# Both halves of the input projection as one sequence, and the squares of x summed on TensorE

## Chip, cores and metric

One core of a Trainium2 chip runs the whole program. The metric is the device time of one execution, in microseconds (us). Of the kernel before there are three timed runs and one execution taken apart by the hardware profiler.

## What is computed

One layer of a decoder for 2048 tokens of width 1024, all in float32. Cut to what the change touches:

```python
u = rms_norm(h, attn_pre_norm)                  # mean of squares over the 1024 features of a token
c_q, c_kv, k_rope, m_q, m_k, m_v, m_o, m_i, m_f = split_cols(u @ w_in, IN_SIZES)
q  = rms_norm(c_q, q_norm) @ w_uq               # low-rank queries: 4 heads of 128 + 64 (rotary)
kv = rms_norm(c_kv, kv_norm) @ w_ukv            # low-rank keys and values
mla_out = causal_mla(q, k, v)                   # softmax attention
hm = mlstm_chunkwise(mq, mk, m_v, m_i, m_f)     # matrix memory with gates
mix = concat(mla_out, sigmoid(m_o) * hm) @ w_out
# residual, a dense gated FFN, a gated per-layer embedding
```

`rms_norm` divides a token's row by the root of its mean square and multiplies by a gain. The product `u @ w_in` is the input projection; the change is in it and in the work beside it.

## The kernel before, in words

Every float32 operand is split into a high and a low part (float32r), and a product is three matmuls, `mm3` (L143, L144, L145: high by high, low by high, high by low). In the trace `xh` and `xl` are the two parts of tokens, `wh` and `wl` those of weights; ScalarE makes the high part (L135), VectorE the low one (L131). `ps` is a PSUM bank of large products, `psx` one of the three banks for small work.

Tokens come in two halves of 1024, each of two blocks of 512. Output rows come in 18 blocks of 128; two row blocks and two token blocks are one pair. A pair is done straight in 96 matmuls of 512 columns, or by Strassen's seven products in 84, for which sums of token operands and of weights are made first. Phase 1 runs so:

- `lead`: the first four row blocks of the first half (the latents), 192 straight matmuls on x that is not yet normalised. Meanwhile the squares of x are added up: ScalarE squares a tile (L264), VectorE adds it to `ct` or `acc` (`square_sum`), and when eight tiles are in, four one-column products with the constant `rmean` give the mean for 512 tokens (`rms_begin`, L169). A chain of eleven small VectorE operations on 128x4 numbers makes the root (L171, L152 to L157), four transposes on TensorE spread it (`rms_end`, L177), ScalarE copies it to `acc`, and the latents are multiplied by it (L720). Only then may the x operands be normalised (`unit`, L641).
- `project(0)`: one straight pair and seven Strassen pairs, 684 matmuls of 512 columns. Beside it `next_stats` adds up the squares of the second half.
- the seam: `lead_first` and `lead_second` load, normalise and sum the second half's x.
- `project(1)`: one straight pair and nine Strassen pairs.

Work beside the products is a list of steps, `side`; one step is taken after each twelve matmuls (`tick`). `beside` is a second list, taken from at every second tick. Steps are `rope_steps` (sines of the positions), `keys_values` (two steps: load, normalise, turn and store a block of the low-rank keys), `query_weights` and `value_weights` (products of weight matrices), and `queries` (20 steps for two token blocks: load, normalise, weights, products, `put` into DRAM, at the end the rotary parts, stored to `q_r`). A scheduler then puts the program into a fixed order for each engine. SP's queue issues nearly all loads and stores, in order. Where a matmul waits, all later ones wait behind it. Tiles come from pools: five of `ld`, four of `wr`, seven of `wh` and of `wl`, one of `sq`.

Phase 2 (attention and mLSTM) follows, with `gates` (scans on the gate rows, which go through DRAM: `g_ag`, `g_ar`, `g_md`, `g_bias`) already started in phase 1. Phase 3 is the FFN. It already has a stream of several halves: the operands of a later half are summed by `x_sums` on VectorE, stored to DRAM (`h1op`) and loaded back by `fed` (L381) as the last pair of the half before needs them no more.

Of the kernel before, what the change touches and what calls it, by code (L numbers as in the profile page):

```python
# [17 lines left out]
P = 128  # L18
D = 1024
T = 2048  # L20
TB = 512
# [41 lines left out]
class Layer:  # L63
# [109 lines left out]

    def along(self, ps, y):
# [29 lines left out]

    def run_later(self):
# [22 lines left out]
    def behind(self):  # L228
        return self.after("PE")

# [175 lines left out]
    def strassen(self, xo, pairs, emit, lead, place=None, late=False):  # L406


        self.stream([self.job(pairs, emit, xo=xo, lead=lead, place=place, late=late)])
# [12 lines left out]
    def stream(self, jobs):  # L422
# [206 lines left out]
    def phase1(self):  # L629
        nc, a, V = self.nc, self.a, self.vecs  # L630
        st = ExitStack()
        with st:
# [13 lines left out]
            def next_x(k, t, alt=False, tag=None):  # L646
                return self.load(a["xT"][k, :, (2 + t) * TB:(3 + t) * TB], alt, tag)

            scale = {}

            def next_stats():
# [15 lines left out]

            self.side = [lambda f=f: behind(f) for f in rest] + 21 * [lambda: None] + self.keys_values(0) + self.query_weights()
            halo = self.project(0, self.ops, None, next_stats(), self.xs)
            self.until(lambda: 1 in scale)  # L670
            get = lambda k, t, tag: unit(next_x(k, t, k >= 4, tag), k, scale[t])
            self.lead_first(get)
            self.lead_second(get)
            self.project(1, self.ops, halo, None, self.xs)

    def lead(self, unit):
# [24 lines left out]
        def arrive(t, k):  # L701
# [4 lines left out]
            if k == 0:  # L706
                acc[t] = self.tl("ct")
            if k or t:
                self.square_sum(acc[t], x, k == 0, tag="acc")

        def begin(t):
            y[t] = self.rms_begin(g, acc[t], 1024)
# [12 lines left out]
        for t in range(2):  # L725
# [5 lines left out]
            for k in range(KD):  # L731
# [6 lines left out]
                for i in range(n):  # L738
                    if t == 0 and k % 4 == 0:
                        w[i, k // 4] = weight(i, k // 4)  # L740
                        if (i, k) == (0, 0):
                            self.square_sum(acc[t], x, True)
# [1032 lines left out]
```

## Time and profile before

| | us |
|---|---|
| median of 3 runs | 2706.18 (2705.91 to 2708.95) |
| the profiled execution | 2700.7 |
| its span in the trace | 2698.9 |
| PE busy | 2572.0 (95%) |
| DVE busy | 1971.9 (73%) |
| ACT busy | 1365.5 (51%) |
| granted clock, mean | 0.978 |

The span leaves 1.8 us of its execution outside; the execution is 5.5 us below the median. PE is TensorE, DVE is VectorE, ACT is ScalarE, POOL is GpSimd, SP is the queue that issues loads and stores. In the slices of the page PE is under 90% in the first five fortieths of the span, in the eighth and ninth, and in the last two. A matmul of 512 columns starts every 0.227 us at the full granted clock.

### The profile page before, as it was taken

Reading aid. Unit: us, or ns where it says so; the run is one execution under the profiler, and the core shown is the slowest. Engines: PE = TensorE matmul, PEld = TensorE weight load, DVE = VectorE, ACT = ScalarE, POOL = GpSimd, SP = SyncE. Lnnn points to the kernel's source line nnn. Section 1 sums busy time; section 2 is a strip of 40 time slices with the busy share of each in tenths; the row PEclk is TensorE's granted clock in tenths of the full one; section 3 lists DMA queues with packets and bytes.
Section 4 is the critical chain, followed back from the end, with each engine's and each line's share of the span. In section 5 each row is a group of like instructions: output and inputs, shape, how many; then the busy total and the mean of one; then the engine's idle time right before and its main releaser. Section 6 shows DMA issues by size and latency. Waiting matters only on the chain.

```text
span 2698.9 us, 36867 instructions
## 1 busy us (share of the span) xinstructions
PE 2572.0 (95%) x12019; PEld 2129.2 (79%) x12019; DVE 1971.9 (73%) x3635; ACT 1365.5 (51%) x2671; POOL 186.1 (7%) x393
## 2 busy tenths in 40 slices
PE   7799889989999999999999999999999999999978
PEld 5678678778888878878888888888888888787867
DVE  8987877566666662799787778676667678877885
ACT  5565565465555553465433354343446445356453
POOL 0010010153333200000000000000000000000000
PEclk9899899999999999999999999999999999999989
DMA  4345444743334133836566578662347567887853
GB/s 144 122 158 192 130 144 147 224 144 102 106 103 110 55 130 113 281 121 223 175 214 224 190 263 288 206 234 94 109 162 233 184 223 266 300 278 250 305 168 97
DMA packets 278845, 486.61 MB, mean 180 GB/s; under 512 B 32476, under 2 KB 54108, under 8 KB 278652
## 3 DMA queue, kind: packets, MB, share of 16 engines
q1 hardware_dynamic: 277308, 483.23, 54.5%
q8 instruction: 94, 1.54, 0.2%
q10 hardware_dynamic: 1344, 1.03, 0.1%
q14 instruction: 99, 0.81, 0.1%
HBM read 321.73 MB, written 162.40 MB: 179 GB/s over the span
## 4 chain that ended last, share of the span: by engine, by line
PE 79%; DMA 8%; DVE 6%; ACT 3%; issue 2%; POOL 1%; SPq 1%; ACTq 0%; DVEq 0%; POOLq 0%
PE ps L143 22%; PE ps L145 21%; PE ps L144 21%; PE ps_t L1400 2%; DMA wr<-g_rd 1%; PE ps_o L144 1%; DVE xl L131 1%; PE ps_s L1360 1%; PE ps_o L145 1%; DVE ct L131 1%; PE ps_o L143 1%; PE ps_s L1361 1%; PE ps_s L1362 1%; PE ps_s L1363 1%; PE psx L143 1%
## 5 line engine op out<-in xcount | busy, mean ns | idle before, releaser
L143 PE MATMUL ps<-xh,wh 128*128 128x512 f32 x2904 | 1141.6, 396 | 61.6 <-ACT wh L135 20.0
L144 PE MATMUL ps<-xl,wh 128*128 128x512 f32 x2904 | 1141.8, 393 | 3.7 <-DVE xl L131 1.9
L145 PE MATMUL ps<-xh,wl 128*128 128x512 f32 x2904 | 1140.2, 393 | 3.8 <-DVE wl L131 3.8
L143 PEld LDWEIGHTS ps<-xh,wh 128*128 128x128 f32 x2904 | 551.7, 190 | 185.9 <-ACT wh L135 21.8
L145 PEld LDWEIGHTS ps<-xh,wl 128*128 128x128 f32 x2904 | 551.0, 190 | 122.6 <-DVE wl L131 6.6
L144 PEld LDWEIGHTS ps<-xl,wh 128*128 128x128 f32 x2904 | 552.3, 190 | 120.5 <-DVE xl L131 3.4
L135 ACT CAST wh<-wr 128x512 fp32r<-128x512 f32 x346 | 214.5, 622 | 325.9 <-PE ps L144 204.1
L131 DVE TENSOR_TENSOR wl<-wr,wh 128x512 fp32r<-128x512 f32 x346 | 238.2, 690 | 157.8 <-ACT wh L135 154.5
L131 DVE TENSOR_TENSOR ct<-ps,ct 128x512 f32<-128x512 f32 x242 | 166.6, 689 | 92.7 <-PE ps L145 89.4
L382 ACT CAST wh<-wl 128x512 fp32r<-128x512 f32 (+1 forms) x217 | 128.3, 594 | 196.5 <-DMA wl<-w_sums_down 114.4
L131 DVE TENSOR_TENSOR wl<-wl,wh 128x512 fp32r<-128x512 f32 (+1 forms) x217 | 140.9, 656 | 100.4 <-ACT wh L382 99.5
L131 DVE TENSOR_TENSOR xl<-xl,xh 128x512 fp32r<-128x512 f32 x234 | 155.3, 689 | 22.8 <-ACT xh L382 21.1
L135 ACT CAST wh<-st 128x512 fp32r<-128x512 f32 x118 | 72.1, 622 | 160.4 <-PE ps L144 104.5
L382 ACT CAST xh<-xl 128x512 fp32r<-128x512 f32 x210 | 128.2, 622 | 42.8 <-DMA xl<-hfop 27.5
L1411 DVE TENSOR_TENSOR acc<-ps_t,acc 128x512 fp32r<-128x512 f32 (+2 forms) x144 | 91.8, 643 | 53.7 <-ACT acc L1410 53.2
L1368 DVE TENSOR_REDUCE mx<-ps_s 128x1 f32<-128x512 f32 (+3 forms) x160 | 97.0, 608 | 36.5 <-PE ps_s L1364 34.2
L467 ACT COPY ct<-ps 128x512 f32<-128x512 f32 x198 | 115.1, 581 | 13.5 <-PE ps L145 13.4
L1410 ACT CAST acc<-ps_t 128x512 fp32r<-128x512 f32 (+2 forms) x144 | 78.1, 552 | 69.5 <-PE ps_t L1400 67.7
L1378 ACT ACTIVATE xl<-ps_s,mn 128x512 f32<-128x512 f32 (+3 forms) x144 | 90.4, 634 | 40.3 <-DVE mn L1374 22.8
L131 DVE TENSOR_TENSOR wl<-st,wh 128x512 fp32r<-128x512 f32 x118 | 80.8, 688 | 11.6 <-ACT wh L135 11.6
L1400 PE MATMUL ps_t<-ident,xl 128*128 128x128 f32 x544 | 88.2, 276 | 0.3 <-DVE acc L1411 0.3
L1568 ACT ACTIVATE ct<-ct 128x512 f32<-128x512 f32 x88 | 55.7, 633 | 51.7 <-DVE ct L131 51.7
(342 smaller groups left out, 3353.5 us busy)
## 6 DMA issues: line engine op xcount, KB each, us to landing
xl<-hfop SPq DMA_DIRECT2D x154, 256.0 KB, 4.8
wl<-w_sums_down SPq DMA_DIRECT2D x112, 256.0 KB, 3.2
wr<-w_gate SPq DMA_DIRECT2D x88, 256.0 KB, 3.1
wr<-w_up SPq DMA_DIRECT2D x88, 256.0 KB, 3.5
wr<-w_in SPq DMA_DIRECT2D x80, 256.0 KB, 3.0
ld<-y SPq DMA_DIRECT2D x56, 256.0 KB, 4.3
wl<-w_sums_ple SPq DMA_DIRECT2D x49, 256.0 KB, 4.3
y<-ct SPq DMA_DIRECT2D x46, 256.0 KB, 3.2
```

The costliest lines, as they stand in the source:

```text
L131: (self.nc.gpsimd if eng == "pool" else self.nc.vector).tensor_tensor(out=out, in0=x, in1=y, op=op)
L135: self.nc.scalar.copy(out=hi, in_=src)
L143: mm(out, w[0], x[0], start=start, stop=False)
L144: mm(out, w[0], x[1], start=False, stop=False)
L145: mm(out, w[1], x[0], start=False, stop=stop)
L382: self.nc.scalar.copy(out=hi[:, :n], in_=raw)
L467: nc.scalar.copy(out=c, in_=bank)
L1368: v.tensor_reduce(mx[:, j, c:c + 1], s_ps[:, :w], axis=AX.X, op=ALU.max, negate=True)
L1378: nc.scalar.activation(out=p[:, :x.shape[1]], in_=x, func=AF.Exp, bias=top, accum_out=sm[:, j, c:c + 1])
L1400: nc.tensor.transpose(t_ps[:, j * P:(j + 1) * P], pt[j, kt // 4][:, kc], self.ident)
L1410: nc.scalar.copy(out=ph[:, b0:], in_=t_ps[:, c0:])
L1411: v.tensor_tensor(pl[:, b0:], t_ps[:, c0:], ph[:, b0:].bitcast(F32), ALU.subtract)
```

## The change

Phase 1 alone changes, in four ways.

1. Squares of x. `mean_square` lets ScalarE square a tile into `sq` and TensorE multiply it by `rmean` at once, four products of one column, added up in PSUM over eight tiles. There are 32 such groups of four instead of 4. VectorE's 28 additions of squares of x are gone. The sums for the latents stay as they were.
2. One sequence. `project` returns a job, and `stream` runs both. The second half has no straight pair and no operands of its own making at the seam: `next_sums` normalises its x, makes the Strassen sums on VectorE (32 large operations), stores 28 tiles of 256 KB in DRAM (`x_op`), and `fed` (L405 in the changed file) loads each back, 14.7 MB in all both ways, in place of the loads of sixteen tiles of x. Twelve matmuls of 512 columns are gone.
3. Finer steps. `keys_values` has six steps, `query_weights` ten and now runs first, `value_weights` one more, and `queries` takes 14 steps for a token block (with pauses 17 for the first half) in place of ten, each issuing less. Idle steps ahead are 14, not 21.
4. The end. What is left of `side` when the sequence is over is run then.

```diff
+    def mean_square(self, st, src, k, n):
+        sq = self.tl("sq")
+        self.nc.scalar.activation(out=sq, in_=src, func=AF.Square)
+        for j in range(4):
+            self.nc.tensor.matmul(st[:, j:j + 1], sq[:, j * P:(j + 1) * P], self.rmean[n], start=k + j == 0, stop=k == KD - 1,
+                                  skip_group_check=True)
...
                 while not jb["ready"]():
-                    if self.side:
-                        self.side.pop(0)()
+                    for work in (self.side, self.beside):
+                        if work:
+                            work.pop(0)()
                     self.run_soon()
                     self.run_later()
...
+            def next_sums(kk):
+                b = [unit(next_x(k, t), k, scale[t]) for k in (kk, 4 + kk) for t in range(2)]
+                self.x_sums(*b, x_op[kk], b[1], self.tl("sq"))
+                fed.append(kk)
+            def scaled(r, t):
+                scale[t] = r
+                if len(scale) == 2:
+                    self.beside += self.spaced([lambda kk=kk: next_sums(kk) for kk in range(4)], 2)
             def next_stats():
                 for t in range(2):
-                    acc = self.acc_tile()
+                    st = self.aux()
                     for k in range(KD):
-                        self.square_sum(acc, next_x(k, t), k == 0, "dve")
-                        yield
-                    self.rms_later(acc, 1024, lambda r, t=t: scale.__setitem__(t, r), lag=3)
+                        self.mean_square(st, next_x(k, t), k, 1024)
+                        if k % 3:
+                            yield
+                    self.rms_soon(st, lambda r, t=t: scaled(r, t))
...
-            self.side = [lambda f=f: behind(f) for f in rest] + 21 * [lambda: None] + self.keys_values(0) + self.query_weights()
-            halo = self.project(0, self.ops, None, next_stats(), self.xs)
-            self.until(lambda: 1 in scale)
-            get = lambda k, t, tag: unit(next_x(k, t, k >= 4, tag), k, scale[t])
-            self.lead_first(get)
-            self.lead_second(get)
-            self.project(1, self.ops, halo, None, self.xs)
+            self.side = [lambda f=f: behind(f) for f in rest] + 14 * [self.idle] + self.query_weights() + self.keys_values(0)
+            first, halo = self.project(0, None, next_stats(), xo=self.ops, lead=self.xs)
+            second, _ = self.project(1, halo, None, feed=lambda i: [x[i] for x in x_op], ready=lambda: len(fed) == 4)
+            self.stream([first, second])
+            while self.side:
+                self.tick()
...
-            if k or t:
-                self.square_sum(acc[t], x, k == 0, tag="acc")
...
+                if k == 0:
+                    acc[t] = self.aux()
+                for kk in [k] if t == 0 else range(2 * k, 2 * k + 2) if k < 4 else []:
+                    self.mean_square(acc[t], x0[kk, t], kk, 1024)
...
-            steps += [lambda: fetch(0), lambda t=t: normalise(t), weight]
+            pause = [] if tb else [self.idle]
+            steps += [lambda: fetch(0), lambda t=t: normalise(t), weight] + pause
             for i0 in range(2):
-                for i in range(2):
-                    steps.append(lambda b=b, i0=i0, i=i: (self.put(product(i), self.q_n[b][2 * i0 + i], tb),
-                                                          fetch(i0 + 1) if i == 0 else weight()))
+                put = [lambda b=b, i0=i0, i=i: self.put(product(i), self.q_n[b][2 * i0 + i], tb) for i in range(2)]
+                steps += [lambda i0=i0: fetch(i0 + 1), *put, weight] + pause
             steps += [lambda t=t: rotary(t, 0), lambda t=t: rotary(t, 1), lambda t=t: rotate(t)]
```

TensorE in the lead, around the transposes that spread the first root (`nrm_y`). Before:

```order
L144 MATMUL ps<-xl,wh 128x512
L145 MATMUL ps<-xh,wl 128x512
L177 MATMUL psx<-ident,nrm_y 128x128 x4
L169 MATMUL psx<-rmean_76,ct 128x1 x4
L143 MATMUL ps<-xh,wh 128x512
```

After:

```order
L144 MATMUL ps<-xl,wh 128x512
L145 MATMUL ps<-xh,wl 128x512
L184 MATMUL psx<-rmean_76,sq 128x1 x12
L190 MATMUL psx<-ident,nrm_y 128x128 x4
L184 MATMUL psx<-rmean_76,sq 128x1 x4
L143 MATMUL ps<-xh,wh 128x512
```

The transposes stand behind 120 large matmuls in both. Now three groups of one-column products, the last of the first block among them, stand right ahead of them.

VectorE, from the first root to the first multiplication of the latents by it (`ct<-ps,acc`). The part of before begins at the root's first operation:

```order
L171 TENSOR_SCALAR nrm_m<-psx 128x4
L131 TENSOR_TENSOR ct<-ct,acc 128x512
L737 SCALAR_TENSOR_TENSOR xl<-ld,vecs,xh 128x512
L1041 SCALAR_TENSOR_TENSOR raw<-raw 128x512
L737 SCALAR_TENSOR_TENSOR xl<-ld,vecs,xh 128x512
L152 TENSOR_SCALAR nrm_y<-nrm_m 128x4
L131 TENSOR_TENSOR ct<-ct,acc 128x512
L131 TENSOR_TENSOR wl<-wr,wh 128x512
L1041 SCALAR_TENSOR_TENSOR raw<-raw 128x512
L154 TENSOR_TENSOR nrm_b<-nrm_y 128x4
```

After:

```order
L131 TENSOR_TENSOR wl<-wr,wh 128x512 x2
L176 TENSOR_SCALAR nrm_m<-psx 128x4
L152 TENSOR_SCALAR nrm_y<-nrm_m 128x4
L154 TENSOR_TENSOR nrm_b<-nrm_y 128x4
L156 SCALAR_TENSOR_TENSOR nrm_b<-nrm_b,nrm_m 128x4
L157 SCALAR_TENSOR_TENSOR nrm_y<-nrm_b,nrm_y 128x4
L154 TENSOR_TENSOR nrm_b<-nrm_y 128x4
```

The large operations that stood inside the chain stand ahead of it or are gone.

TensorE at the end of phase 1. Before, the last products of `queries` (`psx<-raw,acc`) have 60 large matmuls behind them, of which the first rows are:

```order
L143 MATMUL psx<-raw,acc 128x512
L144 MATMUL psx<-raw,acc 128x512
L145 MATMUL psx<-raw,acc 128x512
L143 MATMUL ps<-xh,wh 128x512
L144 MATMUL ps<-xl,wh 128x512
L145 MATMUL ps<-xh,wl 128x512
```

After, eighteen of them stand behind the last large matmul, and phase 2 (`ps_t`, `ps_s`) follows at once:

```order
L144 MATMUL psx<-raw,acc 128x512
L145 MATMUL psx<-raw,acc 128x512
L1273 MATMUL ps_t<-ident,wl 128x128 x4
L1409 MATMUL ps_s<-xh,wh 128x256
L1410 MATMUL ps_s<-xh,wh 128x256
L1409 MATMUL ps_s<-xh,wh 128x256
L1410 MATMUL ps_s<-xh,wh 128x256
```

What stood behind `queries` was the projection; it is the scores of attention (`ps_s`) now, whose `xh` is loaded from `q_n` and `q_r`.

## Rows read from the trace of the kernel before

**Rows 1.** Stretches: from:to, length, busy of each engine (instructions), clock, DMA share, GB/s
```profile
72.00:131.00 59.00, 45.06 (x203) 36.33 (x201) 57.26 (x133) 32.79 (x58) 0.46 (x1) 0.91 0.37 121
200.00:260.00 60.00, 60.00 (x275) 49.63 (x274) 44.21 (x82) 33.24 (x58) 2.37 (x5) 1.00 0.55 176
300.00:320.00 20.00, 7.84 (x22) 5.24 (x21) 19.97 (x34) 9.80 (x18) 0.00 (x0) 0.69 0.19 66
```

**Rows 2.** PE's waits, from the timeline: start, us, instruction, [idle before, releaser]
```profile
48.09 1.11 PE L177 MATMUL psx<-ident,nrm_y 128*128 128x128 f32 x4 [7.08 <-DVE nrm_y L157]
...
168.60 0.33 PE L143 MATMUL psx<-tt,acc 128*128 128x128 f32 x1 [1.46 <-ACT acc L135]
...
170.04 0.33 PE L145 MATMUL psx<-tt,acc 128*128 128x128 f32 x1 [1.01 <-DVE acc L131]
...
307.33 1.22 PE L143 MATMUL ps<-xh,wh 128*128 128x512 f32 x2 [6.01 <-ACT xh L135]
...
318.35 0.80 PE L143 MATMUL ps<-xh,wh 128*128 128x512 f32 x1 [6.15 <-ACT ct L599]
...
370.28 1.09 PE L791 MATMUL psx<-ident,ld 128*128 128x128 f32 x4 [8.04 <-DVE ld L787]
```

**Rows 3.** PE's timeline around one group of four one-column products
```profile
215.10 0.39 PE L145 MATMUL ps<-xh,wl 128*128 128x512 f32 x1
215.32 0.95 PE L169 MATMUL psx<-rmean,acc 128*128 128x1 f32 x8
...
216.46 0.40 PE L144 MATMUL ps<-xl,wh 128*128 128x512 f32 x1
```

**Rows 4.** VectorE's timeline: first and last of six additions of the second half's squares
```profile
109.68 0.69 DVE L131 TENSOR_TENSOR acc<-acc,sq 128x512 f32<-128x512 f32 x1
...
127.73 0.70 DVE L131 TENSOR_TENSOR acc<-acc,sq 128x512 f32<-128x512 f32 x1
```

**Rows 5.** VectorE's timeline: the first root, the second multiplication of the latents, the lead's last operation
```profile
36.92 0.16 DVE L171 TENSOR_SCALAR nrm_m<-psx 128x4 f32<-128x4 f32 x1
...
47.67 0.16 DVE L156 SCALAR_TENSOR_TENSOR nrm_b<-nrm_b,nrm_m 128x4 f32<-128x4 f32 x1
47.87 0.16 DVE L157 SCALAR_TENSOR_TENSOR nrm_y<-nrm_b,nrm_y 128x4 f32<-128x4 f32 x1
...
72.55 2.48 DVE L720 TENSOR_TENSOR ct<-ps,acc 128x512 f32<-128x512 f32 x4 [0.63 <-ACT acc L184]
...
130.43 1.28 DVE L131 TENSOR_TENSOR raw<-ps,ct 128x512 f32<-128x512 f32 x2
```

**Rows 6.** The same mechanism at the FFN's seam: loads (least/median/longest ns), the stretch, its wait
```profile
L381 SPq DMA_DIRECT2D xl<-h1op x28: 319/326/611, 1584.3 to 1620.7; - x28
```
```profile
1584.00:1640.00 56.00, 55.15 (x243) 45.34 (x242) 51.79 (x86) 35.02 (x64) 0.00 (x0) 1.00 0.96 345
```
```profile
1631.28 0.50 PE L145 MATMUL ps<-xh,wl 128*128 128x512 f32 x1 [0.85 <-DVE wl L131]
```

**Rows 7.** Timelines of VectorE and ScalarE at the gates
```profile
360.55 0.18 DVE L1146 TENSOR_TENSOR_SCAN ct<-g_ar 4x16 f32<-4x16 f32 x1 [7.21 <-DMA g_ar<-g_ag]
```
```profile
364.85 1.28 ACT L1161 ACT_TABLE_LOAD   x1 [11.28 <-DMA g_bias<-g_md]
```

**Rows 8.** Timelines at the end of phase 1: PE, SP, ScalarE, GpSimd, PE
```profile
517.19 0.39 PE L143 MATMUL ps<-xh,wh 128*128 128x512 f32 x1
```
```profile
526.95 0.32 SPq L903 DMA_DIRECT2D q_r<-ct  x1
```
```profile
532.74 0.62 ACT L1343 CAST wh<-ld 128x512 fp32r<-128x512 f32 x1 [2.05 <-DMA ld<-q_r]
```
```profile
533.49 1.30 POOL L1344 TENSOR_TENSOR wh<-ld,wh 64x512 fp32r<-64x512 f32 x1 [1.45 <-ACT wh L1343]
```
```profile
528.53 0.50 PE L143 MATMUL ps<-xh,wh 128*128 128x512 f32 x1 [1.99 <-ACT ct L467]
...
535.72 0.28 PE L1360 MATMUL ps_s<-xh,wh 128*128 128x256 f32 x1
```

More of the change, by code (lines that the diff above doesn't have):

```diff
@@ L172, in rms_begin, with rms_root @@
         return self.rsqrt(pool, name, m, [P, 4])
+    def rms_root(self, st, name="nrm"):
+        m = self.g.tile([P, 4], F32, name=name + "_m", bufs=2)
+        self.nc.vector.tensor_scalar(m, st[:, 0:4], EPS, None, ALU.add)
+        return self.rsqrt(self.g, name, m, [P, 4])
+    def mean_square(self, st, src, k, n):
[4 more added lines that the diff above has]
+                                  skip_group_check=True)
     def along(self, ps, y):
@@ L203, in rms_later, with rms_soon, begin @@
             self.defer(lambda: self.soon.append(begin), int(hooks))
+    def rms_soon(self, st, then):
+        def begin():
+            y = self.rms_root(st)
+            self.soon.append(lambda: then(self.rms_end(y)))
+        self.defer(begin)
     def run_later(self):
@@ L229, in behind, with idle @@
         return self.after("PE")
+    @staticmethod
+    def idle():
+        pass
     @staticmethod
@@ L781, in keys_values, with fetch, turn @@
         nc, V = self.nc, self.vecs
+        st = {}
+        def fetch(t):
+            b = 2 * tb + t
+            st[t] = self.load(self.lat_raw[b][2]), self.rms_end(self.y_l[b, "kv"])
         def normalise(t):
-            b = 2 * tb + t
-            x = self.load(self.lat_raw[b][2])
-            r = self.rms_end(self.y_l[b, "kv"])
+            x, r = st[t]
             nc.vector.scalar_tensor_tensor(x, x, V[:, 10:11], r, ALU.mult, ALU.mult)
-            nc.sync.dma_start(out=self.c_n[b], in_=x)
+            nc.sync.dma_start(out=self.c_n[2 * tb + t], in_=x)
+        def turn(t):
+            x, _ = st.pop(t)
             ps = self.aux()
@@ L791, in normalise @@
                 nc.tensor.transpose(ps[:, j * P:(j + 1) * P], x[:, j * P:(j + 1) * P], self.ident)
-            self.put(ps, self.c_t[b], tb)
-        return [lambda: normalise(0), lambda: normalise(1)]
+            self.put(ps, self.c_t[2 * tb + t], tb)
+        return [lambda f=f, t=t: f(t) for f in (fetch, normalise, turn) for t in range(2)]
     def query_weights(self):
@@ L807, in keys, with weight, heads @@
             fetch("w_uqT", 0)
-        def heads(i):
-            w = [self.tl("acc", F32R) for _ in range(2)]
-            self.split(st["raw"], *w)
+        def weight(i):
+            st["w"] = [self.tl("acc", F32R) for _ in range(2)]
+            self.split(st["raw"], *st["w"])
             if i == 0:
                 fetch("w_uqT", 1)
+        def heads(i):
+            w = st["w"]
             ps = self.aux()
@@ L819, in heads @@
             self.put(ps, self.w_qk[:, i * TB:(i + 1) * TB], 0)
-        return [lambda: fetch("w_ukT", 0), keys, lambda: heads(0), lambda: heads(1)]
+        steps = [lambda: fetch("w_ukT", 0), self.idle, keys, self.idle]
+        for i in range(2):
+            steps += [lambda i=i: weight(i), self.idle, lambda i=i: heads(i)]
+        return steps
     def value_weights(self):
@@ L839, in values, with weight @@
             fetch(0)
+        def weight(n):
+            w = st[n] = self.tl("acc", F32R), self.tl("sq", F32R)
+            self.split(st["raw"], *w)
+            fetch(n + 1)
         def product(n):
             h, i = todo[n]
-            w = self.tl("acc", F32R), self.tl("sq", F32R)
-            self.split(st["raw"], *w)
-            fetch(n + 1)
+            w = st.pop(n)
             s = slice(h * P, (h + 1) * P)
@@ L851, in value_weights, with step @@
         first = lambda: st.__setitem__("raw", self.load(a["w_uvT"]))
-        return [first, values] + [lambda n=n: product(n) for n in range(len(todo))]
+        def step(n):
+            product(n)
+            if n + 1 < len(todo):
+                weight(n + 1)
+        return [first, self.idle, values, lambda: weight(0)] + [lambda n=n: step(n) for n in range(len(todo))]
     def queries(self, tb):
@@ L937, in rope_key, with project @@
         nc.sync.dma_start(out=self.k_r[b], in_=kc[0:64])
-    def project(self, tb, xo, halo, stats, lead):
+    def project(self, tb, halo, stats, **how):
         nc, a, g, V = self.nc, self.a, self.g, self.vecs
@@ L1004, in project @@
         w = a["w_in"]
-        self.strassen(xo, [(w[p], w[q]) for p, q in order], emit, lead, place)
-        while tb and self.side:
-            self.tick()
-        return new_halo
+        return self.job([(w[p], w[q]) for p, q in order], emit, place=place, **how), new_halo
     def rope_steps(self):
```

14 lines of the change are left out of this document (5 added, 9 removed).

## The prediction, made before the changed kernel was run

> **What bounds the kernel now.** I read the page's slices first: PE is the engine that fills the span, but not in phase 1, so the stretches of phase 1 come next. In them the reader sees two kinds of time. From 200 to 260 us PE is busy without a gap [rows 1]; an instruction added to PE there is paid in full. From 72 to 131 us it is VectorE that is full (57.26 of 59.00) while PE is idle for 14 us [rows 1]; there a VectorE operation is paid and one on PE is not, as long as nobody waits for it. At 300 to 320 us, the seam between the halves, PE works for 7.84 of 20 us [rows 1]. Then PE's own waits: they are 7.08 us for the first root of the mean square, 1.46 and 1.01 at the weight products, 6.01 and 6.15 at the seam, and 8.04 at the keys [rows 2], together 29.8 us. That is what the change can win at most, with the clock after the waits: the matmul at 318.35 lasts 0.80 where one at 215.10 lasts 0.39 [rows 2, 3], and the 22 records of the seam are busy for 7.84 us where 22 at the full clock are 22 x 60.00/275 = 4.8, so 3.0 us of the seam went there [rows 1].
>
> **The lead.** The price of a group of four one-column products stands in the trace: with one between them, two matmuls with one other between start at 215.10 and 216.46, 1.36 us apart instead of 2 x 0.227, so a group costs 0.90 us [rows 3]. Here a rule can be weighed against the row. The Trainium skill, "TensorE: Matmul & The Clock Gate", on the gap between matmuls issued back to back, states about 25 ns for one of up to 64 columns; the group's eight passes would be 0.2 us by that, an estimate of mine, and the 28 groups more would be some 6 us instead of 25. Without that, by the row: nine groups now stand ahead of the first transposes, which came at 48.09 after large matmuls that ended at 48.09 - 7.08 = 41.0 [rows 2]. All nine on the path would put their end at 41.0 + 9 x 0.90 = 49.1, the three that stand directly ahead of the transposes alone at 43.7; how many of the other six fall into waits that PE has anyway is open, so I take the middle, 46.4. The root's eleven small operations stand 0.20 apart where nothing comes between [rows 5], so 2.2 us, where before they were spread from 36.92 to 48.03 [rows 5]. The transposes come at 48.6, as before: the 7.08 is spent on the groups.
>
> The second transposes then stand behind 216 large matmuls instead of 201, so 3.4 us later, and behind seven more groups, 6.3 us. Before, 72.55 - 48.09 = 24.5 us lay between the first transposes and the latents' second multiplication [rows 2, 5]. After: 48.6 + 24.5 + 3.4 + 6.3, less about 2 that I put on the shorter wait's clock, 80.8, that is 8.3 later than 72.55. From there to 130.43 [rows 5] VectorE is the bound, and six additions of squares go, 0.69 us each [rows 4], 4.1. The lead ends 8.3 - 4.1 = 4.2 later. The ends: -5, if the groups all fall into PE's waits and VectorE alone decides, and +9, if the additions were not on the path.
>
> **The rest of the first half.** Of the sixteen groups of `next_stats` five stand where PE had idle time (before 170 us), and cost nothing; if that cover is gone they cost 4.5. Eleven stand where PE is full: 9.9 us. Two groups of before go, 1.8. That is +8.1. The waits at 168.60 and 170.04 go, since the weights now are split a step or two before the product: -2.5. ScalarE's squares stay the same number; with one buffer `sq`, each waits for the group before, which has 0.90 us to do.
>
> **The seam.** What goes: 6.01 + 6.15 of waits, 3.0 of clock, and 12 matmuls of 0.227, 2.7: 17.9. What is late next is the second half's operands. VectorE makes 32 large operations for them, 22 us at 0.69, in a stretch like 200 to 260 us, where 60.00 - 44.21 = 15.8 us are free [rows 1]; some 6 us do not fit and push VectorE's other work, the low parts of the weights among it. SP's queue gets 28 stores and 28 loads, and whoever is queued behind a store waits until VectorE has made its tile. The extra 14.7 MB in some 100 us are about 150 GB/s on top of 176 [rows 1]. The FFN's seam does the same with 28 loads while 345 GB/s move and VectorE is busy for 51.79 of 56.00, and PE loses 0.85 there, working 55.15 [rows 6]. So the bounds of the new wait are 0.85 and 12.2, the waits that it replaces. I take 3, nearer to the FFN's row, which is the same code. The seam gives 17.9 - 3 = -14.9, with ends of -17 and -6.
>
> **The gates and keys.** The 8.04 us at 370.28 are a wait of PE for the normalised keys [rows 2], but VectorE and ScalarE themselves stand before it, 7.21 for `g_ar` and 11.28 for `g_bias`, two round trips of the gate rows through DRAM [rows 7]. `keys_values` in six steps puts the transposes later than the normalisation, but the operation that waits on the round trip stands in the same two queues still, and the weights' parts wait behind it. I take -2; the ends are 0 and -8.
>
> **The end of phase 1.** Eighteen matmuls of the last `queries` stand behind the last large matmul, and the scores of attention need what comes out of them: rotation on VectorE, a store to `q_r`, a load, a cast, a subtraction. Before, the last of these products was over at 517.19, the `q_r` store was issued at 526.95, the cast ran at 532.74, GpSimd's subtraction at 533.49, and the first scores at 535.72 [rows 8]: 18.5 us. In that time 60 large matmuls ran, 13.6 us of PE; 4.9 us were lost already, of which 1.99 in one wait [rows 8]. After, nothing large is left to run. If the chain takes 18.5 us again the end costs 18.5 - 4.9 = 13.6. If VectorE and ScalarE, with no results of the projection to take up, shorten the first part from 526.95 - 517.19 = 9.8 to some eight operations of 0.69, 5.5, the end costs 9. I take 10, near the lower end, as the two engines are freer. Small waits elsewhere in phase 1 I put at nothing, plus or minus 2.
>
> **The sum.** 4.2 + 8.1 - 2.5 - 14.9 - 2 + 10 = +2.9 us. The profiled execution took 2700.7 us, so 2703.6; the median of the runs lies 5.5 above that execution, so **2709**. Measurements of this kernel tell about 0.2% from no change, 5.4 us, so the forecast is "no difference", on the slow side, between 2701 and 2717 by its own terms.
>
> **Rival 1, faster: the groups and the end are covered.** VectorE alone decides the lead (-5 instead of 4.2), the seam costs as little as the FFN's (-17), and PE has the transposed keys early enough that the gates' wait goes (-8); the end is +9. With 8.1 and -2.5 this is -15.4, so 2691. For it speaks that VectorE is full in the lead [rows 1]; against it that the second transposes must pass seven more groups and that the two gate waits are not moved [rows 7].
>
> **Rival 2, faster: a group costs less than the row says.** The row has one group alone, between two changes of bank. If small passes close up behind one another, a group may cost no more than one large matmul, 0.227 us. The rest of the first half is then 9 x 0.227 = 2.0 and not 8.1, and the lead has nothing of its own but VectorE's gain, -4. The sum is 2.0 - 4 - 2.5 - 14.9 - 2 + 10 = -11.4, so 2695. The 0.90 speaks against it [rows 3]. It is the gap that the Trainium skill's page named above states.
>
> **Rival 3, slower: the one sequence has its seam all the same.** The sums may begin only after both roots, are spaced over eight further ticks, and stand on VectorE between the work of the first half's last pairs. If the last store to `x_op` is issued after the first product of the first half's last pair is done, the loads come too late, SP's queue holds the weights' loads behind them, and PE waits as long as before, 12.2 instead of 3, with the clock's 3.0 on top: 2.9 + 9.2 + 3.0 = +15.1, so 2721. For it speaks that 22 us must find room in 15.8; against it that the order has 228 large matmuls between the last group and that pair, 52 us, of which the spaced ticks take 8 x 12 matmuls, 22 us; 30 are left.
>
> **How the numbers follow.** Forecast 0.47, rival 1 0.20, rival 2 0.08, rival 3 0.25. Of the forecast 0.28 lie within 0.2%, 0.16 above and 0.03 below; rival 1 is faster; rival 2 is faster with 0.06; rival 3 is slower with 0.22. Faster by over 0.2%: 0.29. Within: 0.33. Slower: 0.38. The range of 2693 to 2723 leaves out half of rival 1 and a part of rival 3, 2 in 10.
>
> **What would show it.** In the profile after: groups of one-column products that cost 0.9 us each in the full stretch; first transposes at about 48 and no wait of 7 us; the lead's last operation at about 134 instead of 130.43; no wait over 4 us between the halves; the gates' wait still 5 us or more; and a hole of PE of over 10 us ahead of the first scores. Wrong it would be through the end: if the last `queries` are done well before the last large matmul on the chip, the fixed order notwithstanding, 10 us go; and through the lead, if the squares' single buffer holds ScalarE up.

## The result, and the profile after

| | before | after |
|---|---|---|
| median, 9 runs each | 2702.85 (2699.18 to 2708.95) | 2719.28 (2712.52 to 2721.69) |
| profiled execution | 2700.7 | 2719.28 |
| its span | 2698.9 | 2717.5 |
| PE busy | 2572.0 | 2595.0 |
| DVE busy | 1971.9 | 1959.2 |
| granted clock, mean | 0.978 | 0.977 |

The changed kernel is slower: the ratio is 1.0057, with a 95% interval of 1.0046 to 1.0067. PE is busy for 23 us more, DVE for 13 less, and the span has grown by 18.6 us. Two things said ahead of the result are to be set right here. PE is under 90% in the first two, the fifth, the sixth, the ninth and the last two fortieths of the span before. And the loads of `x_op` do not stand in place of loads of x: both kernels load 48 tiles of x in phase 1, and the changed one loads the second half's sixteen a second time for the sums, only sooner than before. The 28 loads come on top.

The same three stretches as in [rows 1], of the kernel after (columns as there), and the 28 us around PE's longest wait. The clock is the share of the full TensorE clock that was granted:

```profile
72.00:131.00 59.00, 50.41 (x234) 42.07 (x233) 46.91 (x109) 27.84 (x49) 0.00 (x0) 0.85 0.24 82
200.00:260.00 60.00, 46.09 (x212) 37.92 (x210) 52.22 (x93) 27.82 (x45) 3.40 (x7) 0.92 0.69 242
236.00:264.00 28.00, 12.68 (x50) 9.69 (x49) 22.98 (x37) 10.25 (x15) 0.00 (x0) 0.75 0.86 306
300.00:320.00 20.00, 18.04 (x84) 14.64 (x84) 19.92 (x36) 13.85 (x28) 0.00 (x0) 1.00 0.95 318
```

VectorE is no longer full in the lead (46.91 of 59.00). The seam has come out as hoped: PE is busy for 18.04 of 20 us at the full clock. But the stretch that was full before, 200 to 260 us, has lost 13.9 us of PE. PE's waits, as in [rows 2]:

```profile
85.33 1.09 PE L190 MATMUL psx<-ident,nrm_y 128*128 128x128 f32 x4 [2.32 <-DVE nrm_y L157]
...
87.82 0.80 PE L143 MATMUL ps<-xh,wh 128*128 128x512 f32 x1 [1.40 <-DVE ct L749]
...
120.17 0.73 PE L143 MATMUL ps<-xh,wh 128*128 128x512 f32 x1 [3.31 <-ACT ct L488]
...
260.69 1.22 PE L143 MATMUL psx<-raw,acc 128*128 128x512 f32 x2 [14.61 <-ACT raw L135]
...
305.10 0.50 PE L143 MATMUL ps<-xh,wh 128*128 128x512 f32 x1 [1.53 <-ACT ct L488]
...
364.19 1.86 PE L169 MATMUL psx<-rmean,acc 128*128 128x1 f32 x8 [4.46 <-DVE acc L131]
...
552.43 0.58 PE L1409 MATMUL ps_s<-xh,wh 128*128 128x256 f32 x1 [11.65 <-ACT wh L135]
```

To see where the time went I counted the 512-column matmuls of the projection (`ps<-xh,wh` and the two like it) in the order of PE's timeline, and read when the same one starts. From the seam on they are counted from the last one backwards, since after has twelve fewer.

| point | before | after | later by |
|---|---|---|---|
| 230th | 78.11 | 93.27 | 15.2 |
| 400th | 140.08 | 149.40 | 9.3 |
| 740th | 232.02 | 242.07 | 10.0 |
| 780th | 245.32 | 272.33 | 27.0 |
| 876th, last of the first half | 274.93 | 299.74 | 24.8 |
| 740th from the last | 320.22 | 329.50 | 9.3 |
| 550th from the last | 380.27 | 388.65 | 8.4 |
| last | 535.49 | 534.89 | -0.6 |
| first scores of attention | 535.72 | 552.43 | 16.7 |
| end of the span | 2698.9 | 2717.5 | 18.6 |

So the lead costs 9.3 us, the rest of the first half up to the 740th 0.7, the stretch of the second half's sums 14.8, the seam gives 15.5 back, the gates 0.9, the end of phase 1 costs 8.3, and later phases 1.9. The sum is 18.6.

**The long wait.** It stands in none of the places that the prediction had. It is a product of the first half's `queries`, 40 us ahead of the seam. What it waits for, on VectorE, ScalarE and SP of the kernel after:

```profile
253.55 0.68 DVE L131 TENSOR_TENSOR sq<-ld,tt 128x512 f32<-128x512 f32 x1
257.94 0.75 DVE L662 SCALAR_TENSOR_TENSOR ld<-ld,vecs,acc 128x512 f32<-128x512 f32 x1 [3.71 <-DMA ld<-xT]
259.24 1.41 DVE L917 SCALAR_TENSOR_TENSOR ld<-ld,vecs,sq 128x512 f32<-128x512 f32 x2 [0.54 <-ACT sq L197]
```
```profile
258.62 0.59 ACT L197 COPY sq<-psx 128x512 f32<-128x512 f32 x1 [7.97 <-issue]
260.02 1.28 ACT L135 CAST raw<-ld 128x512 fp32r<-128x512 f32 x2 [0.82 <-DVE ld L917]
```
```profile
254.26 0.32 SPq L428 DMA_DIRECT2D x_op<-sq  x1
```

The normalisation of the latents (L917) multiplies by a root that ScalarE copies into `sq` (L197). The pool has one `sq`, and `next_sums` has just put its fourth sum there (253.55), whose store was issued at 254.26. That transfer lands 4.3 us later, and the copy starts then, at 258.62; the page puts its 7.97 us down to "issue", since no instruction that it sees had to end. Ahead of L917 in VectorE's order stands one more operation of the sums (257.94), which waits for a load of x. VectorE waits 0.54 us longer for the copy than for x, so in this order each hides nearly all of the other; the experiments try them one by one.

**The lead.** Nothing stands behind the last squares any more:

```profile
78.09 0.39 PE L145 MATMUL ps<-xh,wl 128*128 128x512 f32 x1
78.32 0.95 PE L184 MATMUL psx<-rmean,sq 128*128 128x1 f32 x8
80.05 1.05 PE L184 MATMUL psx<-rmean,sq 128*128 128x1 f32 x8 [0.78 <-ACT sq L182]
81.88 1.13 PE L184 MATMUL psx<-rmean,sq 128*128 128x1 f32 x8 [0.78 <-ACT sq L182]
...
88.41 0.63 PE L144 MATMUL ps<-xl,wh 128*128 128x512 f32 x1
```

Three groups follow one another 1.78 us apart on average, not 0.90: ScalarE squares into `sq`, TensorE reads it, and only then may ScalarE square again. Then come the root (2.32) and the latents' multiplication (1.40), with no matmul to fill them, and after that the granted clock is 0.50, the lower of its two levels (from 88.41 to 92.60 us; a record of a matmul lasts 0.63 us instead of 0.39).

**The end.** The last eighteen products of `queries` end at about 539.4. SP, of the kernel after:

```profile
544.76 0.34 SPq L953 DMA_DIRECT2D q_r<-ct  x1
...
547.63 0.33 SPq L955 DMA_DIRECT2D q_r<-ct  x1
...
549.70 1.99 SPq L1390 DMA_DIRECT2D ld<-q_r  x4
```

The chain that took 18.5 us beside other work [rows 8] takes 13.0 (539.4 to 552.43) on free engines, and PE is idle through nearly all of it. That what is left of `side` is run at the end is not new, unlike what item 4 of the change says: the kernel before does it too, at the end of its second `project`. What is new is that products of `queries` are left.

### The profile page after: what moved, and what is told of

It reads as the page before. It is cut to its first block, busy times and chain, and to the rows that moved or that the text cites. A ratio compares the mean times of both kernels' runs of the same rounds, so it can differ in the third digit from the quotient of the medians.

```text
span 2717.5 us, 37433 instructions
## 1 busy us (share of the span) xinstructions
PE 2595.0 (95%) x12231; PEld 2156.0 (79%) x12231; DVE 1959.2 (72%) x3612; ACT 1364.6 (50%) x2671; POOL 187.4 (7%) x393
## 4 chain that ended last, share of the span: by engine, by line
PE 82%; DMA 7%; DVE 5%; ACT 2%; issue 2%; POOL 1%; SPq 0%; POOLq 0%; ACTq 0%; DVEq 0%
PE ps L143 22%; PE ps L144 22%; PE ps L145 22%; PE ps_t L1449 2%; DMA wr<-g_rd 2%; PE psx L184 1%; PE ps_o L144 1%; PE ps_s L1409 1%; PE ps_o L143 1%; PE ps_s L1410 1%; PE ps_o L145 1%; PE ps_s L1411 1%; PE ps_s L1413 1%; PE ps_s L1412 1%; PE psx L144 1%
## 5 line engine op out<-in xcount | busy, mean ns | idle before, releaser
L131 DVE TENSOR_TENSOR xl<-xl,xh 128x512 fp32r<-128x512 f32 x256 | 169.2, 685 | 30.8 <-ACT xh L406 29.3
L406 ACT CAST xh<-xl 128x512 fp32r<-128x512 f32 x238 | 144.7, 620 | 59.9 <-DMA xl<-hfop 30.2
L488 ACT COPY ct<-ps 128x512 f32<-128x512 f32 x201 | 116.8, 582 | 15.5 <-PE ps L145 13.6
L1409 PE MATMUL ps_s<-xh,wh 128*128 128x512 f32 (+2 forms) x160 | 67.6, 423 | 20.2 <-ACT wh L135 11.7
```

The source lines that it names most:

```text
L131: (self.nc.gpsimd if eng == "pool" else self.nc.vector).tensor_tensor(out=out, in0=x, in1=y, op=op)
L406: self.nc.scalar.copy(out=hi[:, :n], in_=raw)
L488: nc.scalar.copy(out=c, in_=bank)
L1409: mm(o, qn[0][:, qs], kn[c][0][:, :n], start=True, stop=False)
```

## The experiments

Each run stood beside the kernel before on its own chip, and chips differ: the kernel before had medians of 2694.95, 2695.03, 2693.14 and 2701.9 us in the four comparisons. So ratios to it are compared; 0.001 is 2.7 us. The changed kernel's is 1.0057. A gain against it is the difference of the ratios, and with intervals of 0.001 to 0.0017 either way one under some 5 us is not told from none. Single points of a profile move as well: runs 6 and 9 below, whose ratios are within 0.001 of the changed kernel's and whose lead is the same, stand 1.9 and 2.3 us ahead of it at the 400th matmul (147.55 and 147.06), 2.3 and 2.7 at the 780th and 4.7 and 5.7 at the last.

**1. The fourth sum in a tile of its own** (`own_tile`).

```diff
-                self.x_sums(*b, x_op[kk], b[1], self.tl("sq"))
+                self.x_sums(*b, x_op[kk], b[1], self.tl("s4"))
```

> The changed kernel, but the fourth sum of `next_sums` has a tile of its own (`s4`) and not `sq`, so that the spread root of the first `queries` no longer waits for a store of that sum. Theory A, the one tile `sq` makes PE's wait of 14.61 us before the first product of `queries`: the wait falls to under 4 us and the kernel is 10 to 16 us faster than the changed one, 2704 to 2709. Theory B, the queue and the traffic make it (loads of x and of the latents land late while 347 GB/s move): the wait stays over 9 us and the time falls by less than 6, to 2713 or more.

Ratio 1.0047 (1.0033 to 1.0061). The wait fell from 14.61 to 9.59 us, between the two theories:

```profile
254.00 1.22 PE L143 MATMUL psx<-raw,acc 128*128 128x512 f32 x2 [9.59 <-ACT raw L135]
```

So the tile makes 5 us of it, and 9.6 have another cause. At the 780th matmul the profile is 7.9 us ahead of the changed kernel's, of which 1.7 stood already at the 740th; in the medians the gain, 2.7 us, is not clear. What the 9.6 us end with can be read from VectorE, beside the row of PE's wait (columns as in [rows 1]):

```profile
252.55 0.74 DVE L917 SCALAR_TENSOR_TENSOR ld<-ld,vecs,sq 128x512 f32<-128x512 f32 x1
...
254.92 0.75 DVE L917 SCALAR_TENSOR_TENSOR ld<-ld,vecs,sq 128x512 f32<-128x512 f32 x1 [0.25 <-DMA ld<-lat_raw]
```
```profile
244.40:254.00 9.60, 0.01 (x2) 0.00 (x1) 8.80 (x15) 2.37 (x4) 0.00 (x0) 0.71 0.98 354
```

VectorE is busy for 8.80 of the 9.60 us and comes to the first normalisation without a wait: what is last there is its own order, in which operations of the sums and of the weights stand ahead. The second one waits 0.25 us for its load, so that load came hardly sooner.

**2. The lead's squares on VectorE again** (`lead_dve`): `square_sum` in the lead and `rms_begin` at its end, as before; `next_stats` stays on TensorE.

> The changed kernel with the squares of the lead added on VectorE again, as before; the second half's squares stay on TensorE. Theory A, the groups and the one tile `sq` they share cost the lead 9 us: PE starts the 400th large matmul at about 140, as before, where the changed kernel has 149.4, and the whole is 7 to 11 us faster than the changed one, 2708 to 2712. Theory B, VectorE decides the lead in either form and the groups fall in PE's idle time: the 400th starts at 145 or later and the whole is less than 4 faster.

Ratio 1.0004 (0.9994 to 1.0013), some 14 us faster than the changed kernel and more than either theory had. The 400th matmul starts at 134.03, 15.4 us sooner than in the changed kernel and 6.1 sooner than before. The first root waits as it did before,

```profile
47.77 1.12 PE L190 MATMUL psx<-ident,nrm_y 128*128 128x128 f32 x4 [7.12 <-DVE nrm_y L157]
```

but the 7.76 us that PE lost at 131.17 in the kernel before are gone: VectorE has no squares of the second half to add there. Of the kernel before:

```profile
131.17 0.80 PE L143 MATMUL ps<-xh,wh 128*128 128x512 f32 x1 [7.76 <-DVE raw L131]
```

The change of the lead was a loss of 13 to 15 us (against runs 6 and 9, and against the changed kernel), of which a gain beside it hid some 4 to 6. The long wait is still there in this run, with 16.20 us.

**3. The second half's `queries` in ten steps a block again** (`coarse_end`).

```diff
-                steps += [lambda i0=i0: fetch(i0 + 1), *put, weight] + pause
+                if tb:
+                    steps += [lambda f=put[0], i0=i0: (f(), fetch(i0 + 1)), lambda f=put[1]: (f(), weight())]
+                    continue
+                steps += [lambda i0=i0: fetch(i0 + 1), *put, weight] + pause
```

> The changed kernel with `queries` of the second half in ten steps a block again (a put and a fetch in one step), so that eight steps fewer are left at the end. Theory A, the number of steps left makes PE's hole of 11.65 us ahead of the scores: the last products of `queries` come before the last 40 large matmuls, the hole falls to under 4 us, and the whole is 7 to 12 us faster than the changed one, 2707 to 2712. Theory B, the chain from the last step to the scores is as long wherever the step stands: the hole stays over 9 us and the time is within 3 us of the changed kernel.

Ratio 1.0032 (1.0017 to 1.0047), 6.8 us faster, a little under the lower end. The hole is gone: the last large matmul starts at 540.70, and the scores follow it without a wait, at 540.92, where the changed kernel had 552.43. What is left is a wait of 2.12 us on the way there, as before had 1.99.

**4. The second half's squares on VectorE again** (`stats_dve`): `square_sum` and `rms_later` in `next_stats`; the lead stays on TensorE.

> The changed kernel with the second half's squares added on VectorE again (as before, in the steps of the changed kernel); the lead's squares stay on TensorE. Theory A, eleven groups of 0.90 us each stand where PE is full: 6 to 9 us faster than the changed one, 2710 to 2713, if nothing else waits. Theory B, the groups are hidden behind VectorE there or cost less than the row says: within 3 us of the changed kernel.

Ratio 1.0050 (1.0035 to 1.0065): 1.9 us, not told from nothing. The number is theory B's, its reasons are not. The groups do cost 0.90 us where PE is full (in the kernel after two matmuls with one other and a group between start at 200.29 and 201.65, as in [rows 3]). But without them VectorE holds PE up:

```profile
145.37 0.80 PE L143 MATMUL ps<-xh,wh 128*128 128x512 f32 x1 [8.60 <-DVE raw L131]
```

The 400th matmul starts 4.9 us later than in the changed kernel. What is lost there comes back later: PE's long wait is 7.77 us and one of 2.35, instead of 14.61 and 0.72. The gain and the price of this part cancel.

**5. Two tiles for the squares** (`lead_two_tiles`), in the lead and in `next_stats`.

```diff
-        sq = self.tl("sq")
+        sq = self.tl("s4" if k % 2 else "sq")
```

> The changed kernel, but the squares of x go by turns into two tiles (`sq` and one more). In the lead the groups of the second block took 1.83 us each (0.78 of it a wait for ScalarE's next square), and TensorE's 230th large matmul starts 15 us later than before. Theory A, the one tile makes that: the waits of 0.78 go, the 230th starts 4 to 8 us earlier than in the changed kernel, and the whole gains 3 to 7 us. Theory B, what costs is that the groups and the second root stand on TensorE's path at all (the root's chain of 2.3 us, the latents' multiplication of 1.4, the low clock after them, and VectorE later): two tiles gain less than 3 us, where the squares on VectorE gained some 14.

Ratio 1.0009 (0.9997 to 1.0022), 13 us faster, twice what theory A had. The 230th matmul starts at 79.44, within 1.3 us of the kernel before and 13.8 ahead of the changed one:

```profile
67.34 0.95 PE L184 MATMUL psx<-rmean,sq 128*128 128x1 f32 x8
68.14 1.03 PE L184 MATMUL psx<-rmean,s 128*128 128x1 f32 x8
74.34 0.60 PE L190 MATMUL psx<-ident,nrm_y 128*128 128x128 f32 x4
```

Two groups follow one another 0.80 us apart, and they start over 6 us before the transposes, with large matmuls between. With one tile the squares came late enough that the root had nothing beside it. So it was not the groups' own time that cost, but one tile. The 13 us are not the lead's alone, since `next_stats` has the two tiles too: the profile is 8.4 us ahead of the changed kernel's at the 400th matmul and 12.6 at the 740th. And the long wait is 8.51 us and one of 2.35, though the fourth sum is still in `sq`, so that tile is not all that sets it.

**6. 18 of the 28 stores left out** (`fewer_stores`): the last argument lets `x_sums` store all seven tiles, or the one in `sq` alone.

```diff
-                self.x_sums(*b, x_op[kk], b[1], self.tl("sq"))
+                self.x_sums(*b, x_op[kk], b[1], self.tl("sq"), kk == 0)
...
-feed=lambda i: [x[i] for x in x_op]
+feed=lambda i: [x[i if n == 0 else 5] for n, x in enumerate(x_op)]
```

> The changed kernel without 18 of the 28 stores to `x_op`: of the second to fourth quarter only the sum in `sq` is stored and loaded in place of the other six, so part of the second half is computed from wrong operands. VectorE's work, the loads and the tile `sq` are as in the changed kernel. Theory A, traffic and SP's queue make what the own tile left of the wait before the first product of `queries`: the wait of 14.61 us falls to under 6, and the time by 8 or more. Theory B, the tile `sq` and VectorE's order make it: it stays over 10 us and the time falls by less than 4.

Ratio 1.0053 (1.0037 to 1.0069). The wait hardly moved, while the memory carried far less (240 to 260 us, 192 GB/s and a DMA share of 0.60; the changed kernel had 347 and 0.96 in the same 20 us):

```profile
258.10 1.22 PE L143 MATMUL psx<-raw,acc 128*128 128x512 f32 x2 [13.88 <-ACT raw L135]
```
```profile
240.00:260.00 20.00, 5.46 (x22) 3.70 (x20) 16.44 (x28) 5.49 (x8) 0.00 (x0) 0.71 0.60 192
```

That is theory B. By itself the wait would not exclude the traffic, since the copy into `sq` still comes last. VectorE shows more:

```profile
254.00 1.41 DVE L662 SCALAR_TENSOR_TENSOR ld<-ld,vecs,acc 128x512 f32<-128x512 f32 x2 [2.33 <-DMA ld<-xT]
256.64 1.41 DVE L917 SCALAR_TENSOR_TENSOR ld<-ld,vecs,sq 128x512 f32<-128x512 f32 x2 [1.23 <-ACT sq L197]
```

Without the copy the normalisation could have started at most 1.23 us sooner, since VectorE waits for x with little traffic too. So the traffic of the stores is at most a small part of the cause.

**7. Three parts at once** (`three_mended`): runs 1, 2 and 3 together.

> Three parts at once: the lead's squares on VectorE as before, the fourth sum in a tile of its own, and `queries` of the second half in ten steps a block. If the three gains add up (14, 3 and 7 us in the medians of the chip that showed them), 24 us faster than the changed kernel, some 9 faster than the kernel before, a ratio of 0.997 to it. If the wait before the first product of `queries` grows as the lead gets shorter (16.20 us with the lead on VectorE alone), the gain is under 18 and the ratio 0.999 or more.

Ratio 0.9947 (0.9930 to 0.9964), a median of 2680.66 against 2695.03: faster than both kernels. The gain, 30 us, is more than the 24 that the single ones add up to, but by no more than their intervals allow. The waits left before the first products of `queries`, and what the second of them waits for:

```profile
238.07 1.22 PE L143 MATMUL psx<-raw,acc 128*128 128x512 f32 x2 [8.66 <-ACT raw L135]
...
243.20 0.73 PE L143 MATMUL psx<-raw,acc 128*128 128x512 f32 x2 [1.90 <-ACT raw L135]
```
```profile
241.74 0.75 DVE L919 SCALAR_TENSOR_TENSOR ld<-ld,vecs,sq 128x512 f32<-128x512 f32 x1 [2.57 <-DMA ld<-lat_raw]
```

During the first of them VectorE is busy for 8.22 of 8.66 us, as in run 1; the second is a load of latents.

**8. The sums in half the time** (`three_sums_sooner`): run 7 with `spaced(..., 1)`.

> As the kernel with the three parts, and the four steps of `next_sums` follow one another at every second tick, not at every fourth, so that they are over before `queries` begins. Theory A, the two compete for SP's queue, the `ld` tiles and the memory: apart, the wait before the first product falls under 4 us, and the whole is 6 to 10 us faster than with the three parts, ratio 0.993 to 0.995. Theory B, the sums in half the time need more than the memory gives (11 tiles of 256 KB in some 5 us): PE waits there instead for weights, as long as before, and the ratio stays within 0.001 of the three parts.

Ratio 1.0000 (0.9989 to 1.0010), 14 us slower than run 7. Neither theory: the wait did not stay, it grew.

```profile
248.93 1.22 PE L143 MATMUL psx<-raw,acc 128*128 128x512 f32 x2 [19.22 <-ACT raw L135]
```

In VectorE's order all sixteen normalisations of x now stand ahead of that of the latents, where four stood behind it in run 7. From 220 to 240 us the memory is at 350 GB/s with a DMA share of 0.98, and VectorE is busy for 19.01 of the 20 us:

```profile
242.69 0.75 DVE L662 SCALAR_TENSOR_TENSOR ld<-ld,vecs,acc 128x512 f32<-128x512 f32 x1 [2.79 <-DMA ld<-xT]
...
247.49 0.74 DVE L919 SCALAR_TENSOR_TENSOR ld<-ld,vecs,sq 128x512 f32<-128x512 f32 x1
```

Sums that are issued sooner end little sooner when VectorE and the loads and stores are full (the last of the sixteen normalisations starts at 244.11, in run 7 at 247.44), and `queries` waits for all of them.

**9 and 10. The latents loaded into `ct`** (`latents_in_ct` on the changed kernel, `three_latents_in_ct` on run 7).

```diff
-                x = self.load(self.lat_raw[b][i])
+                x = self.load(self.lat_raw[b][i], not tb)
```

> The changed kernel, but the first half's `queries` load their two latent tiles into `ct` (seven tiles) and not into `ld` (five, of which each step of `next_sums` takes four until its stores have landed). Traffic was excluded: without 18 stores the wait stayed at 13.88 us. Theory A, the wait before the first product of `queries` comes from the queue for `ld` tiles: it falls under 6 us and the time by 6 to 10 from the changed kernel's, ratio to the kernel before 1.002 to 1.0035. Theory B, the shared `sq` alone makes it, since the copy into `sq` is the last to come: the wait stays over 11 us.

> The kernel with three parts mended (ratio 0.9947, a wait of 8.66 us and one of 1.90 left before the first products of `queries`), and the latent tiles in `ct`. If `ld` tiles make what is left, both waits together fall under 3 us and the ratio to 0.991 to 0.993. If VectorE's order makes it (the normalisation of the latents stands behind sums that wait for x), they stay over 7 us and the ratio within 0.001 of 0.9947.

Run 9 has a ratio of 1.0067 (1.0052 to 1.0082) and a wait of 14.71 us: with the one `sq` still shared, the loads change nothing, as theory B had it. Run 10 has 0.9967 (0.9956 to 0.9979), no better than run 7:

```profile
236.19 0.80 PE L143 MATMUL psx<-raw,acc 128*128 128x512 f32 x1 [7.50 <-ACT acc L135]
...
292.20 0.80 PE L143 MATMUL ps<-xh,wh 128*128 128x512 f32 x1 [5.37 <-ACT ct L488]
```

Neither theory holds. The releaser is another now, `acc`, the parts of the weights, whose `ld` tile still stands in the same queue, and the seam has a wait of 5.37 us where run 7 had 0.69. Taking one load out of the queue let the next one be the last.

**11. All squares on TensorE, two tiles, and the other parts** (`all_on_tensor_mended`): run 5 with the own tile's place taken by the second of the two, run 3 and run 9.

> All squares on TensorE as in the changed kernel, but by turns into two tiles; the fourth sum in the second of these; `queries` of the second half in ten steps a block; the latent tiles in `ct`. If the gains of the single runs add up (12 us for two tiles, 7 for the end, 3 to 8 for the wait), 22 to 27 us faster than the changed kernel, a ratio of 0.996 to 0.998 to the kernel before, slower than with the lead's squares on VectorE if TensorE is then the bound of the lead, else as fast.

Ratio 0.9961 (0.9946 to 0.9976), 26 us faster than the changed kernel, as forecast. A wait of 5.60 us is left before the products of `queries` (at 244.61). Run 10, which has the lead's squares on VectorE and the latents in `ct` as well, has 0.9967, not told from it: with two tiles the squares of the lead may stand on either engine.

**12. The sums over before `queries` begins** (`three_stats_sooner`): run 7 with

```diff
-                        if k % 3:
+                        if k % 4 == 3:
                             yield
```

> The kernel with three parts mended, and `next_stats` goes on after every fourth tile of x and not after about every second: the second half's squares are done some 90 large matmuls sooner, and with the same spacing all sixteen tiles of x are normalised before the latents of `queries` on VectorE, where two or three stood behind them. Theory A, the wait before the first products of `queries` (8.66 and 1.90 us with three parts) is there because the sums, as fast as the five `ld` tiles and the memory let them go, are not over when `queries` begins: it falls under 3 us in all, nothing else grows by more, and the ratio to the kernel before is 0.990 to 0.993. Theory B, `queries` waits for its own loads and splits wherever the sums stand: 7 us or more stay, and the ratio is within 0.001 of 0.9947.

The wait is gone: the first products of `queries` follow without one, where run 7 had 8.66 and 1.90 (0.98 us stand at 246.20, before a product of the projection). That half of theory A holds, with a reservation: the last x is normalised at 234.21, 13 us sooner than in run 7, but PE also comes to the 740th matmul 24.8 us later (250.19 against 225.39), and the run does not part the two. But the ratio is 0.9981 (0.9969 to 0.9994), 9 us slower than run 7, since the squares are now crowded and go through the one `sq` again:

```profile
151.91 1.86 PE L184 MATMUL psx<-rmean,sq 128*128 128x1 f32 x8 [1.44 <-ACT sq L182]
...
155.69 1.87 PE L184 MATMUL psx<-rmean,sq 128*128 128x1 f32 x8 [1.91 <-ACT sq L182]
...
180.67 1.08 PE L190 MATMUL psx<-ident,nrm_y 128*128 128x128 f32 x4 [3.44 <-DVE nrm_y L157]
```

The 500th matmul starts at 193.08, in run 7 at 165.42. With two tiles for the squares this version was not tried.

## Why the prediction was right, and where its steps failed

The time lies in the range (2719 in 2693 to 2723) and the sign is the one it put first among the three, but at 0.38 only; the point, 2709, was 10 us short, and its own range of 2701 to 2717 just missed. The forecast sentence, "no difference", did not come true: the interval of the ratio begins at 1.0046. By the sum, +2.9 was forecast for the profiled execution and +18.6 came. That the time lies in the range owes something to the range's width and something to luck: the first two terms below were off by 5.1 and -4.9 us, which cancel.

One reading was wrong at the start. The waits that the change could win were added up to 29.8 us "at most", without PE's waits late in the lead, of 4.48 us at 110.16, 1.87 at 112.83 and 7.76 at 131.17 in the kernel before. Run 2 won the last of them.

- **The lead:** 4.2 forecast, with an upper end of 9; 9.3 measured. The price of a group, 0.90 us, was right [rows 3], and the first transposes came at 49.13 where 48.6 was forecast. What failed is the way from there to the lead's end. That with one `sq` each square waits for the group before, "which has 0.90 us to do", was priced at nothing in the first half's term, and stands in the lead's only at the end, as a sign of being wrong: "if the squares' single buffer holds ScalarE up". That sign came. In the lead and in `next_stats` together the one tile is worth 13 us (run 5). By the runs the lead itself lost 13 to 15, and VectorE's relief, which I had at 4.1, gave 4 to 6 back.
- **The rest of the first half:** 5.6 forecast, 0.7 measured up to the 740th matmul. The groups cost what was said; that VectorE would hold PE up without them (8.60 us in run 4) was not in the sum.
- **The seam:** -17.9 without a new wait forecast, -15.5 measured, with 1.53 us of wait at 305.10 left. The FFN's row [rows 6] was the right one to read for the seam.
- **The price of the sums:** 3 us forecast, 14.8 measured, and this is the term that made the miss. The bounds were 0.85 and 12.2, and I looked for the wait only at the place where the operands are used. I named what does not fit on VectorE, "some 6 us", and what queues on SP, and both are in the wait (runs 1 and 7), but not who else was in the same 30 us: `queries` of the first half, with the same `sq` and the same `ld` tiles. In the FFN's stretch [rows 6] PE has only the large matmuls and no such neighbour, so "the same code" was no proof.
- **The gates:** -2 forecast, -0.9 measured; a wait of 4.46 us stands at 364.19, a little under the 5 that were to show it.
- **The end:** +10 forecast, +8.3 measured, under the lower end of 9. The chain took 13.0 us against the 14.2 of that end, and run 3 shows that the steps left over were the cause.
- **The rivals:** rival 3 had 2721, near the result, for a reason that did not occur; the loads of `x_op` came in time. Rival 2, groups cheaper than the row, is refuted by 200.29 and 201.65, and by the 0.80 us between two groups that stand together (run 5). Rival 1 needed a shorter lead, sums as cheap as the FFN's and no wait at the gates, and none of the three came.

Open in part is what makes the 9 us of wait that the own tile leaves. The traces of runs 1 and 7 show what comes last in them, VectorE's order for the first product (it is busy for nine tenths of the wait) and a load of latents for the second, and in run 10 it is a load of weights. It is hardly the stores' traffic (run 6) and not the latents' loads alone (runs 9 and 10); it is gone when the sums are over before (run 12). No run gave VectorE less to do there, and none gave the loads more `ld` tiles, so how the wait is divided between the two is not shown.

## What to carry to other kernels

Before work is moved to run beside other work, list the small pools that both draw on, not only the engines: one scratch tile, shared by the squares, the fourth sum and the root of `queries`, cost this kernel some 13 us through the squares (run 5) and some 5 of one wait through the sum (run 1; the two may overlap), while the busy shares of the whole span (VectorE 73%) said that there was room. When a product replaces an addition, look at whether the tile between the two engines can be doubled; with one, the two engines took turns here. And fine steps are not free: those that are left when the large products end come out whole (8.3 us here), so count the ticks.

## What the runs showed that was not expected

A store of 256 KB held its tile for some 4.4 us (254.26 to 258.62, while the memory moved 306 GB/s), so a tile shared between a store and an engine was busy far longer than the 0.7 us that VectorE or ScalarE took over it. A group of four one-column products costs 0.80 to 0.90 us at the full clock, about as much as four large matmuls at 0.227; its record lasts 0.95 us there, and 1.86 and 1.87 in run 12, in a stretch (146 to 157 us) whose granted clock was 0.64 on average.
